# Rotary embedding on one core: the load of slab 4 is gated by a memset on VectorE behind slab 1's sum

## The chip, the cores and the metric

The kernel runs on one core of one Trainium2 chip. The metric is the device time of one execution in microseconds (us), taken as the median of several runs. Times inside an execution come from a profiled execution and count from the start of its span.

## The reference

x has 16 batches of 512 rows of 1024 f32 numbers; a row is 16 heads of 64. Each head is rotated with tables cos and sin of 512 rows by 32:

```python
x = x.reshape(batch, seq, num_heads, head_dim)
x1, x2 = x[..., :half_dim], x[..., half_dim:]
rotated = np.concatenate([
    x1 * cos - x2 * sin,
    x1 * sin + x2 * cos
], axis=-1)
```

The tables are the same for every batch and head. Input and output are 33.55 MB each.

## The kernel before

The work is cut into 8 slabs of 2 batches. A slab is a tile of 128 partitions with 8 rows of x each, 8192 f32 per partition, 4 MB in all. A pool of 5 buffers (`slabs`, L41) holds the slabs; `load(s)` (L60) takes the next buffer of the pool and issues the load of slab s at L64. The pool hands its buffers out in turn, in the order of the calls; a sixth call gets the buffer of the first, and whatever writes that buffer first waits until all uses of the old tile are over. Slabs 0 to 5 are loaded from SyncE's queue (SP), slabs 6 and 7 from GpSimd's (POOL).

Slab 0's load is issued at the start (L67), then the two tables are loaded from ScalarE's queue (L76), then slabs 1 to 4 (L80, L81). GpSimd, TensorE and VectorE make from the small tables one bf16 tile `tab` with all that the products need (L84 to L110); this is over before 18 us.

The main loop (L132) runs over passes. Slabs 0, 6 and 7 are done in two passes of half a slab, slabs 1 to 5 in one. A pass has these steps:

- cast (L119, ScalarE): the slab in f32 to `xb` in bf16. `xb` has two buffers, and the cast of the next pass is put ahead of the work of this one (L133, L134).
- two products (L140, VectorE): `xb` by the sine part of `tab` into `t2`, a bf16 view of the slab's own buffer, then `xb` by the cosine part in place.
- the sum (L143, VectorE): `xb` plus `t2` with its halves exchanged.
- copy back (L146, ScalarE): `xb` in bf16 to the slab in f32.
- after the last pass of a slab, the store (L148), issued from ScalarE's queue, and the load of the slab five further on, if there is one (L149, L150).

So slab 5 is loaded into slab 0's buffer when store 0 has landed, slab 6 behind store 1 into slab 1's, slab 7 behind store 2 into slab 2's. Each engine runs its instructions in the order in which the code gives them; an instruction that waits holds all behind it on its engine.

Of the kernel before, what the change touches and what calls it, by code (L numbers as in the profile page):

```python
# [2 lines left out]

# [4 lines left out]


@with_exitstack  # L10
def kernel(
    ctx: ExitStack,
    tc: tile.TileContext,
    x: bass.AP,
    cos: bass.AP,
    sin: bass.AP,
    num_heads: int,
    out: bass.AP,
):
    nc = tc.nc  # L20
    P = nc.NUM_PARTITIONS

    batch, seq, dim = x.shape
    nh = num_heads
    hd = dim // nh
    half = hd // 2
    bf16 = mybir.dt.bfloat16
    f32 = mybir.dt.float32

    nb = 2  # L30
    slots = 5
    nslabs = batch // nb
    rpp = nb * seq // P
    W = rpp * dim
    SP = seq // rpp
    TW = rpp * half

    out_flat = out.rearrange("b s h d -> b s (h d)")

    singles = ctx.enter_context(tc.tile_pool(name="singles", bufs=1))  # L40
    slabs = ctx.enter_context(tc.tile_pool(name="slabs", bufs=slots))  # L41
    xpool = ctx.enter_context(tc.tile_pool(name="xpool", bufs=2))
    psum = ctx.enter_context(tc.tile_pool(
        name="psum", bufs=1, space=bass.MemoryType.PSUM))


    def dram(t, s, a=0, n=W):
        return bass.AP(tensor=t.tensor, offset=t.offset + s * nb * seq * dim + a,
                       ap=[[W, P], [1, n]])


    def view(t, offset, *dims):
        return dataclasses.replace(t, offset=t.offset + offset,
                                   ap=[t.ap[0], *[list(d) for d in dims]])


    slab = {}


    def load(s):  # L60

        queue = nc.sync if s < nslabs - 2 else nc.gpsimd
        slab[s] = slabs.tile([P, W], f32, tag="slab", name="slab")
        queue.dma_start(out=slab[s], in_=dram(x, s))  # L64


    load(0)  # L67


    KQ = 32  # L70
    QS = seq // KQ
    raw = singles.tile([P, 2 * QS * half], f32, tag="raw")
    for i, (eng, src) in enumerate(((nc.vector, cos), (nc.gpsimd, sin))):
        part = raw[:, i * QS * half:(i + 1) * QS * half]
        eng.memset(part, 0.0)  # L75
        nc.scalar.dma_start(out=part[::P // KQ, :], in_=bass.AP(  # L76
            tensor=src.tensor, offset=src.offset,
            ap=[[QS * half, KQ], [1, QS * half]]))

    for s in range(1, slots):  # L80
        load(s)  # L81


    NQ = QS // rpp  # L84
    pick = singles.tile([P, 2 * NQ * P], bf16, tag="pick")
    nc.gpsimd.memset(pick, 0.0)  # L86
    for g in range(2):
        for q in range(NQ):
            part = view(pick, (g * NQ + q) * P + q, (SP, P // SP), (NQ, KQ))
            nc.gpsimd.affine_select(  # L90
                out=part, in_=part, compare_op=mybir.AluOpType.not_equal,
                fill=1.0 - 2.0 * g, base=0,
                pattern=[[0, P // SP], [-(P // KQ), KQ]], channel_multiplier=1)

    tab1 = singles.tile([P, 2 * QS * half], bf16, tag="tab1")
    for i in range(2):
        nc.gpsimd.tensor_copy(out=view(tab1, i * QS * half, (1, QS * half)),  # L97
                              in_=view(raw, i * QS * half, (1, QS * half)))

    acc = psum.tile([P, 2 * rpp * hd], f32, tag="acc")  # L100
    for i in range(2):
        for h in range(2):
            for q in range(NQ):
                nc.tensor.matmul(  # L104
                    view(acc, i * rpp * hd + h * half, (hd, rpp), (1, half)),
                    view(pick, (i * h * NQ + q) * P, (1, P)),
                    view(tab1, i * QS * half + q * TW, (half, rpp), (1, half)),
                    start=q == 0, stop=q == NQ - 1)
    tab = singles.tile([P, 2 * rpp * hd], bf16, tag="tab")
    nc.vector.tensor_copy(out=tab, in_=acc)  # L110

    xb = {}


    def cast(u):
        s, r, n = u
        if r == 0:
            xb[s] = xpool.tile([P, W], bf16, tag="xb", name="xb")
        nc.scalar.copy(out=view(xb[s], r * dim, (1, n * dim)),  # L119
                       in_=view(slab[s], r * dim, (1, n * dim)))  # L120

    passes = []
    for s in range(nslabs):
        n = rpp if 1 <= s < nslabs - 2 else rpp // 2
        passes += [(s, r, n) for r in range(0, rpp, n)]


    cast(passes[0])
    for i, (s, r, n) in enumerate(passes):  # L132
        if i + 1 < len(passes):  # L133
            cast(passes[i + 1])  # L134
        xs = view(slab[s], r * dim, (1, n * dim))
        xu = view(xb[s], r * dim, (1, n * dim))

        t2 = view(slab[s].bitcast(bf16), 2 * r * dim, (1, n * dim))
        for t, a in ((t2, rpp * hd), (xu, 0)):
            nc.vector.tensor_mul(  # L140
                out=t, in0=xu,
                in1=view(tab, a + r * hd, (hd, n), (0, nh), (1, hd)))
        nc.vector.tensor_add(  # L143
            out=xu, in0=xu, in1=view(t2, half, (hd, n * nh), (-half, 2), (1, half)))

        nc.scalar.copy(out=xs, in_=xu)  # L146
        if r + n == rpp:
            nc.scalar.dma_start(out=dram(out_flat, s), in_=slab[s])  # L148
            if s + slots < nslabs:  # L149
                load(s + slots)  # L150


# [1 line left out]
_INS = ['x', 'cos', 'sin', 'num_heads']  # L154
_OUTS = [((16, 512, 16, 64), 'float32')]

_NUMBERS = {'num_heads': 16}


# [26 lines left out]
```

## Time and profile before

| | before |
|---|---|
| median of 3 runs | 162.21 us (162.07 to 162.32) |
| the profiled execution | 162.06 us |
| its span | 160.3 us |
| VectorE (DVE) busy | 109.0 us, 68% |
| ScalarE (ACT) busy | 113.6 us, 71% |
| GpSimd (POOL) busy | 4.4 us |
| TensorE (PE) busy | 1.9 us |
| moved by DMA | 67.24 MB, mean 420 GB/s |
| cast of a whole slab, of a half | 7.02 us, 3.60 us |
| one VectorE operation on a whole slab, on a half | 4.42 us, 2.29 us |
| copy back of a whole slab, of a half | 7.01 us, 3.60 us |

In the profile's lines a group names line, engine, operation and tiles, then partitions by elements; "ACTq", "SPq" and "POOLq" are the queues of these engines, and a DMA line there is the issue of a transfer, not its course. "Landing" is when the whole transfer is done. The figures in square brackets are the idle time of the engine before the instruction and what ended it. In the row of slices each digit is the busy share of a fortieth of the span, in tenths.

The DMA engines serve three queues here: q1 is SP's (loads 0 to 5), q10 ScalarE's (the tables and all stores), q0 GpSimd's (loads 6 and 7).

### The profile page before, as it was taken

Reading aid. Unit: us, or ns where it says so; the run is one execution under the profiler, and the core shown is the slowest. Engines: PE = TensorE matmul, PEld = TensorE weight load, DVE = VectorE, ACT = ScalarE, POOL = GpSimd, SP = SyncE. Lnnn points to the kernel's source line nnn. Section 1 sums busy time; section 2 is a strip of 40 time slices with the busy share of each in tenths; the row PEclk is TensorE's granted clock in tenths of the full one; section 3 lists DMA queues with packets and bytes.
Section 4 is the critical chain, followed back from the end, with each engine's and each line's share of the span. In section 5 each row is a group of like instructions: output and inputs, shape, how many; then the busy total and the mean of one; then the engine's idle time right before and its main releaser. Section 6 shows DMA issues by size and latency. Waiting matters only on the chain.

```text
span 160.3 us, 174 instructions
## 1 busy us (share of the span) xinstructions
PE 1.9 (1%) x8; PEld 1.1 (1%) x8; DVE 109.0 (68%) x35; ACT 113.6 (71%) x23; POOL 4.4 (3%) x14
## 2 busy tenths in 40 slices
PE   0004000000000000000000000000000000000000
PEld 0002000000000000000000000000000000000000
DVE  1000999999989979997996199939559599910000
ACT  3006939998998999899909995199995999280000
POOL 5002000000000000000010001000000000000000
DMA  7999999999999999999999999999999999999994
GB/s 245 417 418 393 499 417 393 474 433 401 384 401 417 474 417 393 474 442 393 458 458 393 450 466 393 433 474 401 417 458 433 393 474 442 393 458 458 393 450 204
DMA packets 2400, 67.24 MB, mean 420 GB/s; under 512 B 288, under 2 KB 288, under 8 KB 352
## 3 DMA queue, kind: packets, MB, share of 16 engines
q10 hardware_dynamic: 1248, 33.69, 48.7%
q1 hardware_dynamic: 864, 25.17, 37.4%
q0 software_dynamic: 288, 8.39, 12.1%
HBM read 33.69 MB, written 33.55 MB: 419 GB/s over the span
## 4 chain that ended last, share of the span: by engine, by line
DMA 49%; ACT 29%; issue 6%; DVE 4%; ACTq 0%; SPq 0%; POOLq 0%
DMA slab<-in_x_dram 28%; DMA out_dram<-slab 21%; ACT slab L146 16%; ACT xb L119 13%; DVE xb L143 1%; DVE xb L140 1%; DVE slab L140 1%; ACTq L148 0%; SPq L64 0%; POOLq L181 0%; ACTq L146 0%; POOLq L64 0%
## 5 line engine op out<-in xcount | busy, mean ns | idle before, releaser
L119 ACT CAST xb<-slab 128x4096 bf16<-128x4096 f32 (+1 forms) x11 | 56.6, 5155 | 24.9 <-DMA slab<-in_x_dram 23.6
L146 ACT CAST slab<-xb 128x4096 f32<-128x4096 bf16 (+1 forms) x11 | 56.6, 5153 | 3.5 <-DVE xb L143 3.5
L140 DVE TENSOR_TENSOR slab<-xb,tab 128x4096 bf16<-128x4096 bf16 (+1 forms) x11 | 35.9, 3260 | 15.4 <-ACT xb L119 15.3
L143 DVE TENSOR_TENSOR xb<-xb,slab 128x4096 bf16<-128x4096 bf16 (+1 forms) x11 | 35.9, 3261 | 0.3
L140 DVE TENSOR_TENSOR xb<-xb,tab 128x4096 bf16<-128x4096 bf16 (+1 forms) x11 | 35.9, 3261 | 0.3
L110 DVE CAST tab<-acc 128x1024 bf16<-128x1024 f32 x1 | 1.2, 1224 | 14.7 <-PE acc L104 14.7
L64 POOL DMA_DIRECT2D slab<-in_x_dram x2 | 1.2, 608 | 84.0 <-DMA out_dram<-slab 84.0
L119 ACT ACT_TABLE_LOAD x1 | 1.3, 1283 | 2.5 <-POOL pick L90 2.5
L104 PE MATMUL acc<-tab,pick 128*128 128x256 bf16 x8 | 1.9, 411 | 14.2 <-POOL tab L97 14.2
L97 POOL CAST tab<-raw 128x512 bf16<-128x512 f32 x2 | 1.2, 611 | 10.9 <-DMA raw<-in_cos_dram 10.9
L104 PEld LDWEIGHTS <-pick 128*128 128x128 bf16 x8 | 1.1, 136 | 14.5 <-issue 12.0
L75 DVE MEMSET raw<- 128x512 f32 x1 | 0.5, 485 | 0.9 <-PEq L167 0.9
L90 POOL TENSOR_SCALAR_AFFINE_SELECT pick<-pick 128x64 bf16<-128x64 bf16 x4 | 0.8, 250 | 0.1
L75 POOL MEMSET raw<- 128x512 f32 x1 | 0.5, 524 | 0.3 <-POOLq L167 0.3
L86 POOL MEMSET pick<- 128x512 bf16 x1 | 0.5, 525 | 0.0
L167 POOL MEMSET const-float32-0.0<- 128x1 f32 x1 | 0.1, 98 | 0.2 <-issue 0.2
L167 POOL MEMSET const-bfloat16-1.0<- 128x1 bf16 x1 | 0.1, 101 | 0.0
L167 POOL MEMSET const-uint8-127<- 128x1 uint8 x1 | 0.1, 101 | 0.0
L167 POOL MEMSET const-float32-1.0<- 128x1 f32 x1 | 0.1, 98 | 0.0
## 6 DMA issues: line engine op xcount, KB each, us to landing
out_dram<-slab ACTq DMA_DIRECT2D x8, 4096.0 KB, 26.8
slab<-in_x_dram SPq DMA_DIRECT2D x6, 4096.0 KB, 27.1
slab<-in_x_dram POOLq DMA_DIRECT2D x2, 4096.0 KB, 23.7
raw<-in_sin_dram ACTq DMA_DIRECT2D x1, 64.0 KB, 8.4
raw<-in_cos_dram ACTq DMA_DIRECT2D x1, 64.0 KB, 11.6
```

Source lines behind the costliest of these rows:

```text
L64: queue.dma_start(out=slab[s], in_=dram(x, s))
L75: eng.memset(part, 0.0)
L86: nc.gpsimd.memset(pick, 0.0)
L90: nc.gpsimd.affine_select(out=part, in_=part, compare_op=mybir.AluOpType.not_equal, fill=1.0 - 2.0 * g, base=0, pattern=[[0, P // SP], [-( ...
L97: nc.gpsimd.tensor_copy(out=view(tab1, i * QS * half, (1, QS * half)), in_=view(raw, i * QS * half, (1, QS * half)))
L104: nc.tensor.matmul(view(acc, i * rpp * hd + h * half, (hd, rpp), (1, half)), view(pick, (i * h * NQ + q) * P, (1, P)), view(tab1, i * QS * ...
L110: nc.vector.tensor_copy(out=tab, in_=acc)
L119: nc.scalar.copy(out=view(xb[s], r * dim, (1, n * dim)), in_=view(slab[s], r * dim, (1, n * dim)))
L140: nc.vector.tensor_mul(out=t, in0=xu, in1=view(tab, a + r * hd, (hd, n), (0, nh), (1, hd)))
L143: nc.vector.tensor_add(out=xu, in0=xu, in1=view(t2, half, (hd, n * nh), (-half, 2), (1, half)))
L146: nc.scalar.copy(out=xs, in_=xu)
L167: nc = _bacc.Bacc("TRN2", target_bir_lowering=False, num_devices=1)
```

## The change

`load` gets an argument: an engine that writes one element per partition of the new tile with a memset ahead of the load. The load writes the same place and so waits for the memset. Slab 4's load is taken out of the loop at the start and put into the main loop, in the pass of slab 1, behind the sum (L143) and ahead of the copy back (L146), with VectorE as its gate. The load of slab 5 stays where it was, behind store 0, in the last pass of slab 0.

```diff
-    def load(s):
+    def load(s, gate=None):
 
         queue = nc.sync if s < nslabs - 2 else nc.gpsimd
         slab[s] = slabs.tile([P, W], f32, tag="slab", name="slab")
+        if gate is not None:
+            gate.memset(slab[s][:, :1], 0.0)
         queue.dma_start(out=slab[s], in_=dram(x, s))
...
-    for s in range(1, slots):
+    for s in range(1, slots - 1):
         load(s)
...
         nc.vector.tensor_add(
             out=xu, in0=xu, in1=view(t2, half, (hd, n * nh), (-half, 2), (1, half)))
+        if s == 1:
+            load(slots - 1, gate=nc.vector)
 
         nc.scalar.copy(out=xs, in_=xu)
```

## The prediction

> **What bounds the kernel now.** I read the page's slices and byte counts first, then the timeline, then the landing times of single transfers. All times are us from the span's start; "cast N" is ScalarE's L119 on slab N (f32 to bf16), "copy N" its L146 (back to f32), "store N" the output transfer issued at L148. Slices and byte count:
>
> ```profile
> DMA  7999999999999999999999999999999999999994
> ...
> HBM read 33.69 MB, written 33.55 MB: 419 GB/s over the span
> ```
>
> The DMA engines are full in all but the first and last slice, while VectorE (68%) and ScalarE (71%) have gaps: 67.24 MB at some 430 GB/s is what the end waits for. So a delay of compute is free as long as it does not empty the transfer queues. How full they are is told by the time from issue to landing of a 4096 KB transfer: slab 0's load (nothing ahead of it), store 0, and store 7 (the last), each from the view of DMA issues in a window that holds this one issue:
>
> ```profile
> slab<-in_x_dram SPq DMA_DIRECT2D x1, 4096.0 KB, 12.8
> ```
> ```profile
> out_dram<-slab ACTq DMA_DIRECT2D x1, 4096.0 KB, 24.0
> ```
> ```profile
> out_dram<-slab ACTq DMA_DIRECT2D x1, 4096.0 KB, 15.0
> ```
>
> 12.8 us is what one such transfer takes in an almost empty machine. Store 0 shares with the loads. The last store takes only 15.0: the queue ahead of it is nearly drained. The cover under which the last store may come late is therefore about 15.0 - 12.8 = 2.2 us. This is the number that decides. Lines of the timeline around the change and at the end:
>
> ```profile
> 37.23 0.35 ACTq L148 DMA_DIRECT2D out_dram<-slab  x1
> ...
> 44.67 4.42 DVE L140 TENSOR_TENSOR slab<-xb,tab 128x8192 bf16<-128x8192 bf16 x1 [0.42 <-ACT xb L119]
> ...
> 58.89 7.02 ACT L146 CAST slab<-xb 128x8192 f32<-128x8192 bf16 x1
> ...
> 65.94 0.34 ACTq L148 DMA_DIRECT2D out_dram<-slab  x1
> 66.32 7.02 ACT L119 CAST xb<-slab 128x8192 bf16<-128x8192 f32 x1 [0.41 <-ACT slab L146]
> ...
> 84.42 7.02 ACT L119 CAST xb<-slab 128x8192 bf16<-128x8192 f32 x1 [4.17 <-DMA slab<-in_x_dram]
> ...
> 144.45 0.34 ACTq L148 DMA_DIRECT2D out_dram<-slab  x1
> ```
>
> VectorE goes from slab 1's sum (ends 44.24) to slab 2 with 0.42 us of idle time. Store 0 is issued at 37.23 and lands 24.0 later, at 61.2; SP, which holds the load of slab 5 for that, agrees:
>
> ```profile
> L64 SPq EVENT_SEMAPHORE  x1: 28/28/28, 61.3 to 61.3; - x1
> L64 SPq DMA_DIRECT2D slab<-in_x_dram x1: 327/327/327, 61.4 to 61.4; - x1
> ```
>
> **What the change really moves.** The pool hands its five buffers out in the order of the calls. That order was 0, 1, 2, 3, 4, 5, 6, 7; it becomes 0, 1, 2, 3, 5, 4, 6, 7, because slab 5's load (behind store 0, in the pass of slab 0) now comes ahead of slab 4's (in the pass of slab 1). So slab 5 gets the free fifth buffer, and slab 4 gets slab 0's. The instruction order of the changed kernel says the same: SP issues five loads in a row without a wait, the fifth now being slab 5's; its sixth, slab 4's, waits for store 0, load 0 and VectorE. And the new memset on VectorE waits for store 0 as well, since it writes the buffer that store 0 reads. It stands between slab 1's sum and slab 2's first product, and VectorE runs in order. So the change is two things: slabs 4 and 5 change places on the load queue, and VectorE stands still until store 0 has landed.
>
> **Step by step.**
>
> *Transfers until 61.* Five loads of 4 MB at the start as before, store 0 at 37.23 and store 1 at 51.58 as before (their copies need slab 1's sum at most). Cost nothing; store 0 lands at 61.2 again.
>
> *The memset.* VectorE is held from 44.24 to 61.3. No row shows this memset on VectorE: it costs at least nothing and at most the 0.485 us of the 128x512 memset at L75; I take 0.1, GpSimd's memsets of 128x1. VectorE then has slab 2's three operations, 3 x 4.42 with 0.03 between: 61.45 to 74.8, where the trace has 58.02. Behind it on VectorE are all later slabs; ScalarE's copy 2 waits for it, and behind copy 2 in ScalarE's order are store 2 and cast 4. Cast 3 (51.97 to 58.99) is ahead of it and unmoved. Copy 2 takes 7.01: 74.9 to 81.9. Store 2 is issued at 81.9, 16 us late; cast 4 could start at 82.3.
>
> *Load of slab 4.* SP issues it behind the memset at about 61.55; nothing is queued behind it on SP. It takes the place of slab 5's load, issued at 61.43, which took 23.0 us beside stores 1 and 2. With the same 23.0 it lands at 84.6, the late end. But store 2's data is no longer beside it after 80. The transfers from 80.5 to 85 by queue (q10 is ScalarE's, q1 SP's, q0 GpSimd's):
>
> ```profile
> q10 hardware_dynamic: 32, 1.05, 53.9%
> q1 hardware_dynamic: 32, 0.52, 27.2%
> q0 software_dynamic: 8, 0.26, 13.5%
> ```
>
> 1.05 MB of store 2, at 430 GB/s 2.4 us, gone: 82.2, the early end. I take the early end: cast 4 at 82.3, with ScalarE and load ready together. Slab 6's load waits for store 1 alone (79.5) and stays at 80.1, so its data fills the queue while store 2 is late.
>
> *From cast 4 on* no load should hold ScalarE: slab 5 has lain ready since 65, slab 6 (issued 80.1) is wanted at 111. So the chain goes at compute speed. Per full slab ScalarE needs 7.02 + 7.01 + the issue and its gap, in the trace 14.35 (cast 3 to cast 4). Cast 4 82.3, store 3 96.3, cast 5 96.65, copy 4 103.7, store 4 110.7, cast 6a 111.1. VectorE's slab 5 starts when cast 5 ends, 103.7, and takes 13.35: 117.05; copy 5 117.15 to 124.15, store 5 124.2. Now half slabs (3.60 each on ScalarE, 3 x 2.29 + 0.07 = 6.95 on VectorE): cast 6b 124.1 to 127.7; copy 6a to 131.2; cast 7a to 134.8; VectorE 6b 127.7 to 134.7; copy 6b to 138.35, store 6 138.4; VectorE 7a 134.85 to 141.8, 7b to 148.85; copy 7b 148.95 to 152.55; store 7 at **152.6**. The trace has 144.45: 8.15 late. The first delay was 16; the 4.17, 5.40 and 1.82 us that ScalarE waited for slabs 5, 6 and 7 and some waits for VectorE pay the other half back.
>
> *Load of slab 7* waits for store 2 to land. From 82 store 2 and slab 6's load share the engines: 8.4 MB at 430 GB/s, 19.5 us, so it is issued at about 103 and, at 23.7 us like before, lands at 127; cast 7a wants it at 131.2. Covered by 4 us.
>
> *The queue at the end.* From 103: store 3, slab 7's load and store 4, 12.6 MB, to about 132; store 5 (issued 124.2) to 142; store 6 (138.4) to 151.5. Store 7 at 152.6 meets an empty queue. It needs 9.7 us at least (the landings of stores 6 and 7 are that far apart, 149.8 and 159.5, with no start to pay) and 12.8 at most (slab 0's load). I take 12.5: slab 0's load shared with 128 KB of tables, 0.3 us. Landing 165.1. The span ends 0.85 after the last landing (160.3 against 144.45 + 15.0), so 165.95; the profiled execution's time is 162.06 for a span of 160.3, so 1.76 more: **167.7**. Beside 162.06 that is +3.5%; the median shown, 162.21, lies 0.15 above the profiled one, which is inside the rounding of this sum.
>
> The slab-0 row of 12.8 may be set beside a rule: the Trainium skill, "DMA: Bandwidth & Descriptors", section "Anatomy of one DMA", fits a transfer issued from GpSimd as 2.0 us fixed plus bytes over 436 GB/s, which by estimate is 11.6 us for 4 MB; store 7 is issued from ScalarE, and by that rule the sum would be 166.8. The same page's "Rules for kernel authors" speaks against the change as its words describe it: issue a transfer early and wait late. The row that bears on it is cast 4, now at 66.32 with no wait for its load.
>
> **Rivals.**
>
> *The gate falls where the words put it (not slower).* Were slab 4 in a free buffer, the memset would cost 0.1 us at 44.3, and its load would go out behind loads 0 to 3 with store 0 (from 37.2) keeping the engines busy; slab 4 would land before 66.3 or little later, and the byte count still sets the end: 161.8 to 162.3. It decides if the memset doesn't wait for store 0. Against it: the allocation order and the named waits. 5%.
>
> *The backlog absorbs the stall (not slower, or faster).* Place: the last store. It holds if store 7 is late by less than 2.2 us, for a time of 161.7 to 162.4; my chain says 8.15, and only another 6 us of slack on ScalarE could change that, where copy 2 to cast 5 has none. 4%.
>
> *Slab 7's load becomes the wait (slower still).* If store 2 took the 37.9 us of store 3, the longest of before, slab 7's load would be issued at 120.3, land at 144, and cast 7a start 12.8 us late: 180.5. Against it: that row is a store queued behind another store; store 2 now has none ahead. 5%.
>
> **Numbers.** Forecast 86%: 167.7. Its own ends: 9.7 us for the last store gives 164.9; cast 4 at 84.6 moves all that follows by 2.3, 170.0, and 0.4 more for a memset at its dearest gives 170.4. That range, 164.9 to 170.4, I give 82%. Less than 0.2% (0.3 us) either way cannot be told from no change here: the two not-slower rivals give 6% there and 3% faster; slower 91%.
>
> **What would show it.** In the changed profile: VectorE idle some 17 us from 44.2, released by the output transfer; slab 2's first product at 61.5; store 2 at 81.9; cast 4 at 82.3 to 84.6; ScalarE with no wait for slabs 5, 6, 7; store 7 near 152.6, 11 to 13 us from landing; a slice or two of thinner DMA near 82 and 152. A memset at 44.3, or store 0 landing far from 61, would make the prediction wrong at its root; a wait at cast 7a would make it too low.

## The result and the profile after

| | before | changed |
|---|---|---|
| median | 162.17 us (162.07 to 162.32, 4 runs) | 166.33 us (166.19 to 166.56, 4 runs) |
| profiled execution, its span | 162.06 us, 160.3 us | 166.19 us, 164.4 us |
| ratio, 95% interval | | 1.0255 (1.024 to 1.027) |
| VectorE, ScalarE busy | 109.0, 113.6 us | 108.9, 113.6 us |
| moved by DMA | 67.24 MB | 67.24 MB |

The changed kernel is slower by 4.2 us, 2.6%. No engine works longer; the time is waiting. (Lines of the changed kernel are numbered 2 to 4 higher: cast L121, products L142, sum L145, copy back L150, store L152, the memset L65, the load L66.)

The page of the changed kernel, slices and two groups:

```profile
DVE  1000999999700009999996999799991999991000
ACT  3006949998999930007999999998599999937000
...
DMA  7999999999899999999989999999899998996885
GB/s 247 407 399 502 391 431 454 391 502 383 375 399 438 446 391 486 407 430 454 375 271 430 446 391 502 391 407 478 383 502 391 407 486 383 494 399 271 383 383 255
...
L150 ACT CAST slab<-xb 128x4096 f32<-128x4096 bf16 (+1 forms) x11 | 56.6, 5154 | 21.9 <-DVE xb L145 21.9
...
L65 DVE MEMSET slab<- 128x1 f32 x1 | 0.1, 59 | 17.1 <-DMA out_dram<-slab 17.1
```

VectorE has four empty slices in a row, ScalarE three just behind them. The DMA row is full while both stand still; its dents come later, behind 82 us (271 GB/s) and from 148 on (271 GB/s with a 6, then 8, 8, 5). The memset itself takes 59 ns; ahead of it VectorE waited 17.1 us for an output transfer. ScalarE's copies wait 21.9 us in all for VectorE's sums (3.5 before), 15.85 of them at copy 2.

The same in the timeline of the changed kernel (start, duration, what, and in brackets the idle time before and what ended it):

```profile
61.38 0.06 DVE L65 MEMSET slab<- 128x1 f32 x1 [17.15 <-DMA out_dram<-slab]
61.45 4.43 DVE L142 TENSOR_TENSOR slab<-xb,tab 128x8192 bf16<-128x8192 bf16 x1
...
74.83 7.02 ACT L150 CAST slab<-xb 128x8192 f32<-128x8192 bf16 x1 [15.85 <-DVE xb L145]
...
81.88 0.34 ACTq L152 DMA_DIRECT2D out_dram<-slab  x1
82.26 7.02 ACT L121 CAST xb<-slab 128x8192 bf16<-128x8192 f32 x1 [0.41 <-DMA slab<-in_x_dram]
...
152.44 0.34 ACTq L152 DMA_DIRECT2D out_dram<-slab  x1
```

Slab 2's first product begins at 61.45 where it began at 44.67; store 2 goes out at 81.88 in place of 65.94; cast 4 begins at 82.26 in place of 66.32; store 7 goes out at 152.44 in place of 144.45. What store 7 then meets is seen in the DMA share of the stretch from 150 to 154 (the columns are the stretch, its length, the busy time of PE, PEld, DVE, ACT and POOL, the clock, the DMA share and GB/s), and in its landing:

```profile
150.00:154.00 4.00, 0.00 (x0) 0.00 (x0) 0.00 (x0) 2.41 (x1) 0.00 (x0) 1.00 0.34 147
```
```profile
out_dram<-slab ACTq DMA_DIRECT2D x1, 4096.0 KB, 11.1
```

The engines were at a third: store 6 was nearly through and store 7 not yet there. In the same stretch the kernel before has a share of 1.08:

```profile
150.00:154.00 4.00, 0.00 (x0) 0.00 (x0) 0.00 (x0) 0.00 (x0) 0.00 (x0) 1.00 1.08 467
```

From its issue store 7 needs 11.1 us, so it lands at 163.5, and the span ends 0.9 later.

### The profile page after: what moved, and what is told of

Same layout as the page of the kernel before. It is cut to its first block, busy times and chain, and to the rows that moved or that the text cites. A ratio compares the mean times of both kernels' runs of the same rounds, so it can differ in the third digit from the quotient of the medians.

```text
span 164.4 us, 176 instructions
## 1 busy us (share of the span) xinstructions
PE 1.9 (1%) x8; PEld 1.1 (1%) x8; DVE 108.9 (66%) x36; ACT 113.6 (69%) x23; POOL 4.4 (3%) x14
## 2 busy tenths in 40 slices
DMA packets 2400, 67.24 MB, mean 409 GB/s; under 512 B 288, under 2 KB 288, under 8 KB 352
## 4 chain that ended last, share of the span: by engine, by line
ACT 37%; DMA 28%; DVE 20%; issue 6%; ACTq 0%; SPq 0%; DVEq 0%
ACT slab L150 22%; ACT xb L121 15%; DMA out_dram<-slab 15%; DMA slab<-in_x_dram 13%; DVE slab L142 7%; DVE xb L145 7%; DVE xb L142 7%; ACTq L152 0%; SPq L66 0%; ACTq L150 0%; DVE slab L65 0%; DVEq L65 0%
## 5 line engine op out<-in xcount | busy, mean ns | idle before, releaser
L150 ACT CAST slab<-xb 128x4096 f32<-128x4096 bf16 (+1 forms) x11 | 56.6, 5154 | 21.9 <-DVE xb L145 21.9
L121 ACT CAST xb<-slab 128x4096 bf16<-128x4096 f32 (+1 forms) x11 | 56.6, 5154 | 14.3 <-DMA slab<-in_x_dram 12.7
L142 DVE TENSOR_TENSOR slab<-xb,tab 128x4096 bf16<-128x4096 bf16 (+1 forms) x11 | 35.9, 3259 | 6.4 <-ACT xb L121 6.2
L142 DVE TENSOR_TENSOR xb<-xb,tab 128x4096 bf16<-128x4096 bf16 (+1 forms) x11 | 35.9, 3261 | 0.3
L145 DVE TENSOR_TENSOR xb<-xb,slab 128x4096 bf16<-128x4096 bf16 (+1 forms) x11 | 35.9, 3261 | 0.3
L65 DVE MEMSET slab<- 128x1 f32 x1 | 0.1, 59 | 17.1 <-DMA out_dram<-slab 17.1
L66 POOL DMA_DIRECT2D slab<-in_x_dram x2 | 1.2, 611 | 90.0 <-DMA out_dram<-slab 90.0
```

What stands on the lines that cost most here:

```text
L121: nc.scalar.copy(out=view(xb[s], r * dim, (1, n * dim)), in_=view(slab[s], r * dim, (1, n * dim)))
L142: nc.vector.tensor_mul(out=t, in0=xu, in1=view(tab, a + r * hd, (hd, n), (0, nh), (1, hd)))
L145: nc.vector.tensor_add(out=xu, in0=xu, in1=view(t2, half, (hd, n * nh), (-half, 2), (1, half)))
```

## The experiments

Each kernel was timed together with runs of the kernel before, whose median was 162.2 to 162.3; ratios stand against those. "Theory" below is this: the price comes from slab 4's tile getting slab 0's buffer, which holds VectorE (through the memset) and slab 4's load until store 0 has landed; the later issue by itself costs nothing, as long as the transfer queues stay filled.

### The gate without the shared buffer (own_buffer)

```diff
-    slabs = ctx.enter_context(tc.tile_pool(name="slabs", bufs=slots))
+    slabs = ctx.enter_context(tc.tile_pool(name="slabs", bufs=slots - 1))
+    own = ctx.enter_context(tc.tile_pool(name="own", bufs=1))
...
-        slab[s] = slabs.tile([P, W], f32, tag="slab", name="slab")
+        pool = own if s == slots - 1 else slabs
+        slab[s] = pool.tile([P, W], f32, tag="slab", name="slab")
         if gate is not None:
-            gate.memset(slab[s][:, :1], 0.0)
+            gate.tensor_copy(out=slab[s][:, :1], in_=xb[s - 3][:, :1])
```

> The gate as the words of the change have it, without the shared buffer: slab 4 has a buffer of its own, slabs 0 to 3 and 5 to 7 turn in four, and the gate on VectorE copies one element per partition out of slab 1's sum, so that it can't come ahead of it. The memset's wait for store 0 is gone, the later issue of slab 4's load (about 44.3) stays. My theory (the cost is VectorE's stall and the exchange of slabs 4 and 5, both from the buffer): 162.0 to 162.5, like the kernel before. Rival (a load issued later costs by itself): 165 or more, with cast 4 waiting for its load.

Measured: 162.29 us, ratio 1.0007 (0.9998 to 1.0015). Its timeline:

```profile
44.21 0.15 DVE L67 CAST slab<-xb 128x1 f32<-128x1 bf16 x1
44.39 13.63 SPq L68 DMA_DIRECT2D slab<-in_x_dram  x2
...
44.61 4.42 DVE L144 TENSOR_TENSOR slab<-xb,tab 128x8192 bf16<-128x8192 bf16 x1 [0.25 <-ACT xb L123]
...
68.64 7.02 ACT L123 CAST xb<-slab 128x8192 bf16<-128x8192 f32 x1 [2.73 <-DMA slab<-in_x_dram]
...
91.59 7.02 ACT L123 CAST xb<-slab 128x8192 bf16<-128x8192 f32 x1 [9.01 <-DMA slab<-in_x_dram]
...
147.42 0.34 ACTq L154 DMA_DIRECT2D out_dram<-slab  x1
```

The load is issued behind slab 1's sum, just as the change says in words, and costs nothing measurable. It is not that nothing is late: ScalarE waits 2.73 us for slab 4 and 9.01 for slab 5 (before, cast 4 had only the 0.41 behind copy 2 and no wait for its load, and cast 5 waited 4.17), and store 7 goes out at 147.42, 3.0 us later than in the kernel before. The store queue covers that: store 7 lands 12.0 us after its issue, in place of 15.0, and the span is 160.3 again. The rival, that a late issue costs by itself, is out for this kernel and a delay of this size.

### The exchange alone (swap_only) and the stall alone (stall_only)

swap_only has no gate; slab 4's load is issued behind slab 5's, in the pass of slab 0:

```diff
-        if s == 1:
-            load(slots - 1, gate=nc.vector)
...
             if s + slots < nslabs:
                 load(s + slots)
+                if s == 0:
+                    load(slots - 1)
```

> Slab 5's load takes the fifth buffer and slab 4's waits for store 0, as in the changed kernel, but with no gate, so VectorE is not held. Theory A (the stall of VectorE alone makes the cost): 162.0 to 162.5. Theory B (either of the two is enough, since ScalarE's cast 4 then waits for a load that lands near 84.4, and copy 3 and store 3 stand behind cast 4): store 2 at 66 as before, cast 4 at 84.4, store 7 at 154.6, landing 11.1 later, 168.3.

stall_only loads slab 4 early, and gates slab 5's load, which is in slab 0's buffer by the old order:

```diff
-    for s in range(1, slots - 1):
+    for s in range(1, slots):
         load(s)
...
         if s == 1:
-            load(slots - 1, gate=nc.vector)
+            load(slots, gate=nc.vector)
...
-            if s + slots < nslabs:
+            if 0 < s and s + slots < nslabs:
                 load(s + slots)
```

> Slab 4 is loaded early as in the kernel before; the gate sits on slab 5's load, at the same place of VectorE, so that VectorE is held until store 0 has landed and the order of the slabs is that of before. Theory B (the stall alone is enough): the same chain as in the changed kernel, store 2 at 81.9, cast 4 at 82.3, 166.3. Rival (what costs is that slab 4 comes late): 162.0 to 162.5.

Measured: swap_only 168.67 us, ratio 1.0421 (1.0384 to 1.0458); stall_only 166.43 us, ratio 1.0257 (1.0244 to 1.027). The timeline of swap_only:

```profile
65.92 0.34 ACTq L150 DMA_DIRECT2D out_dram<-slab  x1
...
84.68 7.02 ACT L121 CAST xb<-slab 128x8192 bf16<-128x8192 f32 x1 [18.79 <-DMA slab<-in_x_dram]
91.61 7.01 ACT L148 CAST slab<-xb 128x8192 f32<-128x8192 bf16 x1
91.73 4.43 DVE L142 TENSOR_TENSOR slab<-xb,tab 128x8192 bf16<-128x8192 bf16 x1 [19.39 <-ACT xb L121]
```

and of stall_only:

```profile
61.69 0.06 DVE L65 MEMSET slab<- 128x1 f32 x1 [17.62 <-DMA out_dram<-slab]
...
82.19 0.34 ACTq L152 DMA_DIRECT2D out_dram<-slab  x1
82.57 7.02 ACT L121 CAST xb<-slab 128x8192 bf16<-128x8192 f32 x1 [0.41 <-ACT slab L150]
```

Either part is enough, and they do not add. With the stall alone cast 4 begins at 82.57, with the exchange alone at 84.68, in the changed kernel, which has both, at 82.26. What follows cast 4 takes the same 70.2 us to store 7's issue in all three. The exchange alone is 2.3 us worse than both together (168.67 against 166.33), about the 2.4 us between their casts 4: store 2 goes out at 65.92 there and shares the engines with slab 4's load, which in the changed kernel has no store beside it from 80 on.

So of VectorE's 17 us none would come back if only the memset were taken out: the wait for slab 4's load stands right behind it, at a higher price.

### One slab earlier (gate_behind_slab0) and one later (gate_behind_slab2)

The edit to the changed kernel is the condition alone; the first is the first plus line, the second the other:

```diff
-        if s == 1:
+        if s == 0 and r + n == rpp:
             load(slots - 1, gate=nc.vector)
```
```diff
-        if s == 1:
+        if s == 2:
             load(slots - 1, gate=nc.vector)
```

> The same memset and load, one slab earlier: behind slab 0's sum and ahead of slab 5's load, so that the buffers go round in the old order and the memset waits for no store. In VectorE's order it falls between slab 1's two products, near 35. My theory (the price is the buffer's, not the gate's): 162.0 to 162.5. Rival (a gate on VectorE and a load behind it cost by themselves): 163 or more.

> The same memset and load, one slab later: behind slab 2's sum. Now slab 6's load also comes ahead of slab 4's and takes slab 0's buffer, and slab 4 takes slab 1's, so the memset waits for store 1 (79.5). My theory: VectorE held from 58 to 79.6, slab 4's load issued at 79.8 and landed near 100 beside store 2, cast 4 there, all that follows 70.2 later as in the changed kernel (store 7 at 170.7), the time 183 to 186. Rival (only how late the gate is counts, one slab is 14.35 us and most of it is covered): 168 to 172.

Measured: 162.15 us, ratio 0.9996 (0.9984 to 1.0008), and 185.55 us, ratio 1.1433 (1.1411 to 1.1455). The timeline of gate_behind_slab2:

```profile
78.43 0.06 DVE L65 MEMSET slab<- 128x1 f32 x1 [20.47 <-DMA out_dram<-slab]
...
78.52 0.33 SPq L66 DMA_DIRECT2D slab<-in_x_dram  x1
...
101.36 7.02 ACT L121 CAST xb<-slab 128x8192 bf16<-128x8192 f32 x1 [35.51 <-DMA slab<-in_x_dram]
...
171.54 0.34 ACTq L152 DMA_DIRECT2D out_dram<-slab  x1
```

The same memset and the same load cost nothing, 4.2 and 23.3 us as the gate goes back by one slab each time. What differs is whose store the buffer waits for: nobody's, store 0 (61.3), store 1 (78.4). Cast 4 at 101.36 plus 70.2 is store 7's issue at 171.54, plus 11.1 and the 2.7 of the end 185.3.

### Half stores at the end (changed_half_stores, before_half_stores)

Slabs 6 and 7 go out by halves, from SP's queue, in the changed kernel and in the kernel before:

```diff
-        if r + n == rpp:
+        if s >= nslabs - 2:
+            nc.sync.dma_start(out=dram(out_flat, s, r * dim, n * dim), in_=xs)
+        elif r + n == rpp:
             nc.scalar.dma_start(out=dram(out_flat, s), in_=slab[s])
+        if r + n == rpp:
```

> The changed kernel with slabs 6 and 7 stored by halves, from SP's queue, each half as soon as it is copied. The first half of slab 7 can then go out at 145.3 and fill the gap of some 2.2 us between stores 6 and 7. My theory (the engines ran dry for 2.2 us near 152, for 0.5 near 82, and moved a little less in between, and all of this is lost time): only the gap near 152 comes back, 164.0. Rival (only the length of the last transfer counts, 152.4 plus a start of 1.4 and half of 9.7): 161.5. Rival (the end is set by something else): 166.3.

> The kernel before with slabs 6 and 7 stored by halves from SP's queue. Its engines do not run dry before the end, so there is nothing to fill: 161.8 to 162.5. Rival (half stores shorten the end of any of these kernels): 161.5 or less.

Measured: changed_half_stores 165.58 us, ratio 1.0201 (1.0188 to 1.0214); before_half_stores 162.63 us, ratio 1.0025 (1.0014 to 1.0035). From 150 to 154 changed_half_stores has

```profile
150.00:154.00 4.00, 0.00 (x0) 0.00 (x0) 0.00 (x0) 2.36 (x1) 0.00 (x0) 1.00 0.97 414
```

so the gap is filled, yet only 0.8 us came back, not the 2.3 I expected. Another 3.4 us were lost elsewhere, where I had counted 1.8. The stretch from 80 to 84.4 in the changed kernel, and after it that of the kernel before, shows one place:

```profile
80.00:84.40 4.40, 0.00 (x0) 0.00 (x0) 4.37 (x2) 3.99 (x2) 0.69 (x1) 1.00 0.90 320
```
```profile
80.00:84.40 4.40, 0.00 (x0) 0.00 (x0) 4.37 (x2) 0.25 (x1) 0.69 (x1) 1.00 1.02 439
```

In the kernel before, half stores cost 0.4 us (0.25%), a little over what I allowed. Why was not tried; that end has no gap to fill.

### Slabs 6 and 7 from SP's queue (changed_half_sp, changed_sp, before_sp)

```diff
-        queue = nc.sync if s < nslabs - 2 else nc.gpsimd
+        queue = nc.sync
```

> The changed kernel with the half stores, and slabs 6 and 7 loaded from SP's queue and not from GpSimd's. Theory (in the changed kernel slab 6's load runs alone near 82, and GpSimd's load starts slowly there: the engines moved 320 GB/s from 80 to 84.4 and 420 up to 123, against 439 and 435 before, 2.5 us in all): half of it or more comes back, 164.0 to 164.8, against 165.6 with GpSimd's loads. Rival (any load that starts on an empty machine loses this, whichever queue): 165.3 to 165.8.

> The changed kernel with slabs 6 and 7 loaded from SP's queue, and whole stores. Theory (the changed kernel has two ends close together: store 7's issue at 152.4 plus 11.1, and the bytes with what was lost near 82 behind them; the first is the later one): the lost transfer time comes back but only widens the gap ahead of store 7, so 166.0 to 166.5 as before. Rival (the loss near 82 is a part of the 4 us): 165.3 or less.

> The kernel before with slabs 6 and 7 loaded from SP's queue. If GpSimd's slow start costs only where its load runs alone, there is nothing to gain here, since store 2 runs beside slab 6's load: 162.0 to 162.5. Rival (GpSimd's loads cost in any case): 161.7 or less, which would beat both kernels.

Measured: changed_half_sp 164.21 us, ratio 1.0126 (1.0102 to 1.015); changed_sp 166.44 us, ratio 1.0259 (1.0244 to 1.0273); before_sp 162.4 us, ratio 1.0003 (0.9993 to 1.0013). Of changed_half_sp:

```profile
80.00:84.40 4.40, 0.00 (x0) 0.00 (x0) 4.37 (x2) 3.99 (x2) 0.00 (x0) 1.00 1.12 454
84.40:123.00 38.60, 0.00 (x0) 0.00 (x0) 36.13 (x10) 35.30 (x6) 0.00 (x0) 1.00 0.99 421
```

and of changed_sp:

```profile
80.00:84.40 4.40, 0.00 (x0) 0.00 (x0) 4.37 (x2) 3.99 (x2) 0.00 (x0) 1.00 1.09 462
```

From SP's queue slab 6's load leaves the engines no pause (454 GB/s in place of 320) and 1.4 us come back; the edit moves slab 7's load too, so they are the worth of both. That is seen only with half stores. With whole stores (changed_sp) nothing comes back: there the end is store 7's issue plus 11.1, whatever the engines did earlier, and the time won only lies idle ahead of store 7. The changed kernel thus has two ends close behind each other, the chain through store 7 and the bytes with the time lost near 82. And where store 2 runs beside slab 6's load, as in the kernel before, GpSimd's queue costs nothing (before_sp).

These runs do not show that GpSimd as the issuer is the cause. On SP's queue slab 6's load goes out at 79.6 (changed_sp) in place of 80.27, and stands behind slab 4's load, whose data still runs, on the same queue; so it never starts on empty engines. A load that does is slow from SP's queue too. The first 4.4 us from the issue of slab 0's load (SP's queue, the kernel before, nothing ahead of it), and from that of slab 7's load in gate_behind_slab2 (GpSimd's queue, no other data moving), are

```profile
0.74:5.14 4.40, 0.00 (x0) 0.10 (x1) 0.48 (x1) 1.28 (x1) 1.81 (x6) 1.00 0.90 320
```
```profile
100.65:105.05 4.40, 0.00 (x0) 0.00 (x0) 0.00 (x0) 3.69 (x1) 0.53 (x1) 1.00 0.76 246
```

The rival that any load starting on an empty machine loses time, whichever queue it comes from, is therefore not out: no run starts the same load from both queues on empty engines.

The 421 GB/s up to 123, against 435 before, did not go away. The engines send their packets nearly in step, 0.52 MB each round of 1.2 us (in slices of 0.6 us from 61 on the kernel before moves 55 and 819 GB/s in turn), so a round more or less at the edges of a stretch moves such a figure; I can't tell how much of it is real. changed_half_sp stays 2.0 us over the kernel before, and that rest is open.

## Why the prediction was right

*What the change moves*: right. The memset waited for store 0, VectorE stood from 44.2 to 61.4, and slab 4 was loaded into slab 0's buffer behind slab 5. own_buffer and gate_behind_slab0 take the buffer out of it and are back at 162.2. The rival at 5%, that the gate falls where the words put it, had the right price (161.8 to 162.3, measured 162.29) for a kernel that this one is not.

*The memset*: 0.06 us, taken as 0.1. Slab 2's first product: 61.45, as stated.

*Load of slab 4*: between the early and the late end I took the early one, 82.2. Issued at 61.5, it landed 20.6 later, at 82.1. swap_only shows the late end: 84.68.

*From cast 4 on*: 82.26 (82.3 stated), store 5 at 124.08 (124.2), store 7 at 152.44 (152.6). The reason given for the half that is paid back was not exact: the three waits for loads sum to 11.4 us, and only 8 come back, because ScalarE waits 2.5 us for VectorE at copy 5 (117.03), which is new, and about 0.4 us behind a copy stays ahead of casts 5 and 6.

*Load of slab 7*: the cover was thinner than stated. Store 2 landed 22.9 after its issue, at 104.8, slab 7's load went out at 105.37 and landed 24.4 later, at 129.8; cast 7a began at 130.97. I had given the cover 4 us, it was 1.2. The transfers near 82 were slower than 430 GB/s, and this I had not seen; in changed_sp, without that loss, store 2 landed at 102.2. The third rival, that slab 7's load becomes the wait, was thus 1.2 us away, though its 180.5 was far.

*The queue at the end*: store 6 landed at 153.6, not by 151.5, so store 7 was issued 1.1 us ahead of that. Its last packets were few (33 GB/s from 150 to 152), and store 7 took no longer for them than with nothing beside it.

*The last transfer*: the term that was mis-sized. I took 12.5 us for store 7 alone, from slab 0's load; it took 11.1, and 11.1 again for stores 6 and 7 of swap_only and store 7 of gate_behind_slab2. A load is a poor row for a lone store, and not only at the start of the kernel: slab 7's load, alone in gate_behind_slab2, took 12.5. 152.44 + 11.1 + 0.85 + 1.76 is 166.15, the profiled time 166.19; 1.4 of the 1.5 us between it and 167.7 are this term. The fit from the Trainium skill that I set beside it ("DMA: Bandwidth & Descriptors", "Anatomy of one DMA"), 11.6 by estimate, was nearer than my row, and 0.5 us too long for this store from ScalarE's queue; for that load of slab 7, which GpSimd issued, it is 0.9 us too short.

*The cover of the last store* was therefore not 2.2 us but 15.0 - 11.1 = 3.9. own_buffer bears that out: 3.0 us of delay at store 7 went by unnoticed. The second rival (the backlog absorbs the stall) fails all the same, since 8.0 is more than either.

*The skill's rule "issue early, wait late"* ("Rules for kernel authors" of the same page), which I named as speaking against the change: own_buffer issues slab 4's load at 44.4, some 41 us later (the kernel before has issued all of its first five loads by 3.3), at a ratio of 1.0007. In this kernel, whose transfer queues are full, an early issue bought nothing.

## What to carry to other kernels

When a load is moved in a kernel with a rotating pool, first write down which buffer each tile gets and whose last use it must wait for; here one exchange of two calls turned a harmless 59 ns gate into a wait for a 4 MB store, on the engine that everything else needs. In a kernel bound by DMA, estimate the free delay as the landing time of the last store less that of a lone one (3.9 us here). Below it lateness cost nothing, above it nearly all counted: store 7 issued 3.0, 8.0, 10.4 and 27.1 us later (own_buffer, the changed kernel, swap_only, gate_behind_slab2) made the kernel 0.1 (inside the noise), 4.2, 6.5 and 23.3 us slower. Where two waits stand behind each other, take each out alone before believing either: here each alone kept the whole cost.

## What the runs showed of the hardware

A load that starts with no other data moving starts slowly: over the 4.4 us from its issue 320 GB/s from SP's queue (slab 0 in the kernel before) and 246 from GpSimd's (slab 7 in gate_behind_slab2), against 357 for a lone store (store 7 there). In the changed kernel slab 6's load, from GpSimd's queue, comes when slab 4's is ending, and the stretch from 80 to 84.4 moves 320 GB/s; issued from SP's queue behind slab 4's it moves 462 (changed_sp), which was worth 1.4 us once nothing else hid it. Beside a store there is no such loss (439 GB/s in the kernel before). How much of it the issuing engine makes is not shown.

A lone 4 MB store takes 11.1 us: so did stores 3 to 7 of gate_behind_slab2, with nothing beside them, and the last store of the changed kernel, swap_only, stall_only and changed_sp. Of these 9.7 are the transfer at full rate (the distance of the landings of stores 6 and 7 in the kernel before). The first load of the kernel takes 12.8.
